# Attention's value products as one stream per pair of heads over the gate projections, half sums, and dependent loads issued later

## The chip, the cores and the metric

The kernel runs on one core of a Trainium2 chip. A core has five engines that work from queues of their own and meet through semaphores: TensorE (PE; its weight loads are listed apart as PEld), VectorE (DVE), ScalarE (ACT), GpSimd (POOL) and SyncE (SP). SP issues most of the DMAs; POOL issues a few. An engine runs its queue in order: whatever stands behind a waiting instruction waits too. The metric is the device time of one execution in microseconds (us); lower is better.

## The reference

The program is one decoder block on a sequence of 1024 tokens with 1024 features, in float32: an RMS norm with modulation, two token mixers side by side (chunkwise retention, and dilated window attention), a gated merge, and a squared-ReLU MLP. The change concerns the attention. There are three groups of heads with different dilation, four heads each, of width 128:

```python
ATT_GROUPS = ((128, 1), (512, 4), (2048, 16))
...
s = (einsum('bhrnid,bhrnjd->bhrnij', qs, kb) * (dh ** -0.5) + bias)
mx = max(s); e = exp(s - mx); den = sum(e)
p = e / den
lse = mx + log(den)
o = einsum('bhrnij,bhrnjd->bhrnid', p, vb)
...
wts = softmax(stack(lses), axis=0)
att = einsum('gbhs,gbhsd->bshd', wts, o_all)
att_out = att @ w_att_out
merged = sigmoid(gate_a) * ret_out + sigmoid(gate_b) * att_out
```

So the outputs of the three groups are weighted by a softmax over the groups' log sums, per token and head, and added. `gate_a` and `gate_b` are projections of the same normed input as queries, keys and values.

## The kernel before, in words

**Arithmetic.** Each float32 product is made of three products of parts in the shorter float32r format: a high part (a rounded copy, ScalarE) and a low part (the difference, VectorE). `mm3` (L195) issues low by high, high by low, high by high (L200, L202, L204). A weight is split by `split_w` (L190 on ScalarE, L191 on VectorE).

**Steps.** From the attention on, the work is a list of steps (`Steps`, L69). Each step has weights to load, which are issued on SP's queue (L84) as slots of a ring of three raw tiles come free, and a body. Before an ordinary step's body the weights of the next one or two steps are split; a step marked `manual` calls for that itself, at the place where its body says so. The instructions of every engine stand in the order in which the Python code emits them.

**Attention.** The heads are done in two pairs (`pair` 0 and 1); `g` is the group and `a` the head of the pair. For each pair come six key steps (`att_step`, L1692; order of groups 1, 2, 0), then gate projections as cover (`cover_step`, L1728): gates 0 to 3 for pair 0, gates 4 to 6 for pair 1, and gate 9 in `gate_step` (L1778) at the end. Every key step and gate step holds one projection of 8 chunks of six matmuls with 512 columns, into one PSUM tile of two banks (tiles `ak` and `gate`). Between the chunks lie other products:

- the scores of the previous (g, a), added to the bias into the tile `P` (L1469), their maximum, and the exponential with its sum (L1492);
- for each finished group 1 and 2, `stats_out` (L1545): the row statistics are stored in DRAM in the group's token order (`std`, L1550) and loaded back in natural order (`stn`, L1551). The load waits, on SP's queue, until the store has landed;
- after the last scores, in the first gate step, `weights` (L1553): the softmax over groups. The weights of groups 1 and 2 go through DRAM in the same way (`wtd`, L1577; `wg`, L1579). `pscale` (L1582) multiplies P by them, five of eight blocks on VectorE (L1587) and three on ScalarE (L1589);
- the products with the values. `pv_tr` (L1600) transposes up to four blocks of P on TensorE (tile `pt`, L1604) and splits them (`pth` L1608 on ScalarE, `ptl` L1609 on VectorE); `pv_mm` (L1611) multiplies by the value parts (L1628 to L1630) into an accumulator `pv`, a PSUM tile of two banks; `pv_end` (L1632) adds the accumulator into P's place (copy L1637 for group 0, add L1641 for the others) and splits the final sum for the output projection (L1646, L1647).

Projection tiles and accumulators share two PSUM tiles of two banks (`ps_mm`), so that a new accumulator waits until the one before has been read. `v_fetch` (L1515) loads the values of a group, `v_split` (L1521, L1522) splits them.

`pv` (L1650) is a generator that keeps three transposed blocks ahead of the products. `weave_pv` (L1676) sets a projection's chunks between its parts. Before the change each group is woven on its own: pair 0 has group 0 in gate 2, group 1 in gate 3, group 2 in the first key step of pair 1; pair 1 has group 0 in gate 6, and groups 1 and 2 in gate 9. The sigmoid of a gate (L1759) reads its PSUM tile at the end of its own step and is stored in DRAM (L1760).

Beside the first pair of heads, POOL's queue sums retention results from DRAM to DRAM (`result_sums`, L589): eight transfers of 2 MB, one after the other.

Of the kernel before, what the change touches and what calls it, by code (L numbers as in the profile page):

```python
# [133 lines left out]
def block_kernel(ctx, tc, io, stop=None, dbg=None):  # L134
# [677 lines left out]
    def wsplit(ap):  # L812
        return ap, split_w
# [528 lines left out]
                      [wsplit(w) for w in r_loads.get((h, c), ())], manual=True)  # L1342


    A = {}
    att_ctx = ExitStack()
    right_ctx = ExitStack()

# [196 lines left out]
    def stats_out(pair, g):  # L1545

        if g == 1:
            A["stn"] = A["p"].tile([P, 3, 8, 4], F32, tag="stn", name=f"stn{pair}")
        d = dram.tile([S, 4], F32, name=f"std{pair}{g}")
        nc.sync.dma_start(natural(d, g, 4), blocks(A["st"][:, g], g))  # L1550
        nc.sync.dma_start(A["stn"][:, g], natural(d, 0, 4))  # L1551

    def weights(pair):  # L1553

        p, st = A["p"], A["st"]
        stn = [st[:, 0], A["stn"][:, 1], A["stn"][:, 2]]
        mx = p.tile([P, 8, 2], F32, tag="mx", name=f"mx{pair}")
        wt = p.tile([P, 3, 8, 2], F32, tag="wt", name=f"wt{pair}")
        pr = p.tile([P, 3, 8, 2], F32, tag="pr", name=f"pr{pair}")
        sm = p.tile([P, 8, 2], F32, tag="ssum", name=f"ssum{pair}")  # L1560
        wg = p.tile([P, 2, 8, 2], F32, tag="wg", name=f"wg{pair}")
        nc.vector.tensor_max(mx, stn[0][:, :, 0:2], stn[1][:, :, 0:2])
        nc.vector.tensor_max(mx, mx, stn[2][:, :, 0:2])
        for g in range(3):
            nc.vector.tensor_sub(wt[:, g], stn[g][:, :, 0:2], mx)
        nc.scalar.activation(wt, wt, AF.Exp)
        for g in range(3):
            nc.vector.tensor_mul(pr[:, g], wt[:, g], stn[g][:, :, 2:4])
        nc.vector.tensor_add(sm, pr[:, 0], pr[:, 1])
        nc.vector.tensor_add(sm, sm, pr[:, 2])  # L1570
        nc.vector.reciprocal(sm, sm)
        for g in range(3):
            nc.vector.tensor_mul(wt[:, g], wt[:, g], sm)
        A["w", 0] = wt[:, 0]
        ds = [dram.tile([S, 2], F32, name=f"wtd{pair}{g}") for g in (1, 2)]
        for g in (1, 2):
            nc.sync.dma_start(natural(ds[g - 1], 0, 2), wt[:, g])  # L1577
        for g in (1, 2):
            nc.sync.dma_start(blocks(wg[:, g - 1], g), natural(ds[g - 1], g, 2))  # L1579
            A["w", g] = wg[:, g - 1]  # L1580

    def pscale(g, a):  # L1582
# [46 lines left out]
            nc.tensor.matmul(o, v[0], pl[:, cs], start=False, stop=False, skip_group_check=True)  # L1629
            nc.tensor.matmul(o, v[0], ph[:, cs], start=False, stop=True, skip_group_check=True)  # L1630

    def pv_end(pair, g, a, acc):  # L1632

        f = flat(acc)
        sumt = A["P", 0, a][:, :1024]
        if g == 0:
            nc.scalar.copy(sumt, f)  # L1637
        else:
            r = 4 * g
            sv = sumt.rearrange("p (i r) -> p r i", r=r)  # L1640
            nc.vector.tensor_add(sv, f.rearrange("p (r i) -> p r i", r=r), sv)  # L1641
# [8 lines left out]
    def pv(pair, *groups):  # L1650


        items = [(g, a, bank) for g in groups for a in range(2) for bank in PT[g]]
        accs = {}
        queue = []

        def mm(g, a, bank, pt):
            if (g, a) not in accs:
                accs[g, a] = (ps_mm(f"pv{pair}{g}{a}"), set())
            pv_mm(g, a, bank, pt, *accs[g, a])  # L1660
            if bank is PT[g][-1]:
                pv_end(pair, g, a, accs[g, a][0])
                return True
            return False

        for item in items:
            if item[2] is PT[item[0]][0]:
                del A["scaled", item[0], item[1]]
            queue.append((*item, pv_tr(pair, *item)))
            yield item is items[2]  # L1670
# [5 lines left out]
    def weave_pv(main, n, pair, *groups):  # L1676


        parts, waits = sum(4 * len(PT[g]) for g in groups), 2 * len(groups) + 1
        heavy = max(1.0, (parts - waits) / max(1, n - waits))  # L1680
        total = parts + waits * (heavy - 1)
        done = share = 0
        for wait in pv(pair, *groups):
            share += heavy if wait else 1
            while done * total < share * n:
                next(main, None)
                done += 1
        drain(main)

    combos = [(g, a) for g in (1, 2, 0) for a in range(2)]  # L1690

    def att_step(pair, i):  # L1692

        g, a = combos[i]

        def body(*args):
            ps = ps_mm(f"ak{pair}{i}")
            gen = proj_gen(ps, hd.pop("w") if i == pair == 0 else args[-1])
            if i == len(combos) - 1:
                v_fetch(pair, 0)  # L1700
            if i > 0:
                last = combos[i - 1]
                weave(gen, NK, scores_gen(pair, *last), len(SB[last[0]]), lag=2)
            elif pair == 0:
                args[0](1, True)
                for _ in range(4):
                    next(gen)
                on_T(H - 1, NC - 2)
                on_T(H - 1, NC - 1)
                drain(gen)  # L1710
                u_final(H - 1)
                result_sums()
                open_att()
                args[0](3)
            else:

                weave_pv(at(gen, 0, lambda: v_split(0, 2)), NK - 1, 0, 2)
            if i == 0:
                A["st"] = A["p"].tile([P, 3, 8, 4], F32, tag="st", name=f"st{pair}")
                bias_load(pair)  # L1720
            k_split(pair, g, a, ps)
            if i > 0:
                scores_end(pair, *last)
                if last[1] == 1:
                    stats_out(pair, last[0])
        return body

    def cover_step(pair, n):  # L1728


        i = COVER[pair][n]

        def body(*args):
            ps = ps_mm(f"gate0{i}")
            gen = proj_gen(ps, args[-1])
            if n == 0:
# [22 lines left out]
            nc.scalar.activation(t, flat(ps), AF.Sigmoid)  # L1759
            nc.sync.dma_start(gate_d[i], t)  # L1760
        return body

    for pair in range(2):
        for i, (g, a) in enumerate(combos):
            steps.add(att_step(pair, i),
                      ([] if i == pair == 0 else [wsplit(io["w_ak"][g * 4 + 2 * pair + a])]) +
                      ([(aq_d[pair, *combos[i - 1]], q_prep(pair, *combos[i - 1]))] if i > 0 else []),
                      manual=i == pair == 0)
        for n in range(len(COVER[pair])):
            more = [(aq_d[pair, *combos[-1]], q_prep(pair, *combos[-1]))] if n == 0 else []  # L1770
            steps.add(cover_step(pair, n), more + [wsplit(io["w_gate"][len(COVER[0]) * pair + n])], manual=n == 2)
# [26 lines left out]
    steps.add(gate_step, [wsplit(io["w_gate"][len(COVER[0] + COVER[1])])])  # L1798

    def open_mh():  # L1800
        hpool_ctx.close()
# [883 lines left out]
```

## Time and profile before

| | us |
|---|---|
| median of 3 runs | 2212.76 |
| lowest, highest run | 2210.62, 2216.35 |
| the profiled execution | 2214.49 |
| its span (first to last instruction) | 2212.6 |
| TensorE busy in the span | 2157.9 |
| VectorE busy | 1472.7 |
| ScalarE busy | 944.8 |

Times in the profile are counted from the span's start. The key steps of pair 0 begin at 954 us, its gate steps at 1035.8, gate 2 after 1060.6; the key steps of pair 1 follow from 1111, its gate steps from 1199.8, and the output projection of the attention (tile `ao`) from 1280.1. A row of the timeline gives start, duration, engine, line, operation, output and inputs, and in brackets the idle time before it and what ended it. A line SPq is the moment at which SP issues a DMA, not the transfer. In the page, the granted clock is that of TensorE, 1.00 being full speed.

### The profile page before, as it was taken

The numbers are of one execution on the slowest core, as the hardware profiler recorded it, in microseconds if no ns is written. First come the engines' busy times: TensorE is split into PE (matmuls) and PEld (weight loads), VectorE is DVE, ScalarE is ACT, GpSimd is POOL, SyncE is SP. The second block draws the span as 40 slices with busy tenths as digits, with TensorE's granted clock in tenths as the row PEclk, the third lists the DMA queues.
The fourth block names the chain that finished last, engine by engine and source line by source line (L and its number), as shares of the span: only waits on it lengthen the run. The fifth ranks groups of instructions, "written<-read, shape, count | busy, mean of one in ns | idle before, by whom it ended". The sixth has DMA issues, their size and how long they took to land.

```text
span 2212.6 us, 27000 instructions
## 1 busy us (share of the span) xinstructions
PE 2157.9 (98%) x10034; PEld 1787.3 (81%) x10034; DVE 1472.7 (67%) x2271; ACT 944.8 (43%) x1709; POOL 169.2 (8%) x176
## 2 busy tenths in 40 slices
PE   7999999999999999999899999999999999999998
PEld 4888888888788788888788788888878888788887
DVE  6756777766566677754555644676876665787855
ACT  4532323333234466654534634524454445533412
POOL 0100111000001233300000000002100000000003
PEclk9999999999999999999999999999999999999999
DMA  9869999744687645569523265654154445645322
GB/s 383 222 208 294 293 304 278 200 153 151 222 298 289 227 158 190 176 216 259 166 79 105 87 214 186 238 179 164 38 191 148 147 147 183 250 135 175 119 86 77
DMA packets 159906, 422.54 MB, mean 191 GB/s; under 512 B 27478, under 2 KB 55389, under 8 KB 155358
## 3 DMA queue, kind: packets, MB, share of 16 engines
q1 hardware_dynamic: 151902, 372.57, 47.5%
q0 software_dynamic: 7872, 48.24, 9.4%
q8 instruction: 79, 1.29, 0.2%
q14 instruction: 53, 0.43, 0.1%
HBM read 325.71 MB, written 160.32 MB: 220 GB/s over the span
## 4 chain that ended last, share of the span: by engine, by line
PE 85%; DVE 6%; ACT 4%; DMA 3%; issue 1%; POOL 0%; SPq 0%; POOLq 0%; DVEq 0%; ACTq 0%
PE qap L200 6%; PE qap L204 6%; PE qap L202 6%; PE fp L200 4%; PE fp L202 4%; PE fp L204 4%; PE f2a L202 2%; PE f2a L204 2%; PE f2a L200 2%; PE ak L200 2%; PE ak L202 2%; PE ak L204 2%; PE va L202 1%; PE va L204 1%; PE va L200 1%; PE rg L202 1%
## 5 line engine op out<-in xcount | busy, mean ns | idle before, releaser
L200 PE MATMUL qap<-hh,qaw 128*128 128x512 f32 x264 | 102.9, 390 | 0.2 <-DVE qat L291 0.2
L202 PE MATMUL qap<-hl,qaw 128*128 128x512 f32 x264 | 102.7, 389 | 0.0
L204 PE MATMUL qap<-hh,qaw 128*128 128x512 f32 x264 | 102.7, 389 | 0.0
L631 POOL TENSOR_TENSOR j<-qk,j 128x512 fp32r<-128x512 f32 x32 | 50.5, 1579 | 326.4 <-ACT j L630 326.4
L2140 ACT ACTIVATE a<-a 128x512 f32<-128x512 f32 x48 | 30.3, 632 | 79.3 <-DVE a L2139 79.3
L2036 POOL TENSOR_TENSOR accnf<-accnf,sqnf 128x256 f32<-128x256 f32 (+1 forms) x18 | 16.6, 922 | 613.3 <-ACT sqnf L2035 613.3
L1492 ACT ACTIVATE P<-P,ng 128x128 f32<-128x128 f32 (+1 forms) x96 | 41.9, 438 | 41.5 <-DVE ng L1489 41.5
L200 PEld LDWEIGHTS qap<-hh,qaw 128*128 128x128 f32 x264 | 49.6, 188 | 11.1 <-DVE qat L291 0.9
L204 PEld LDWEIGHTS qap<-hh,qaw 128*128 128x128 f32 x264 | 49.6, 188 | 10.4
L202 PEld LDWEIGHTS qap<-hl,qaw 128*128 128x128 f32 x264 | 49.6, 188 | 10.3
L2329 ACT CAST w2h<-w2s 128x512 fp32r<-128x512 f32 x36 | 22.4, 622 | 79.0 <-DVE w2s L2367 79.0
L257 DVE TENSOR_TENSOR fw<-w1r,fw 128x512 fp32r<-128x512 f32 x48 | 32.9, 688 | 33.3 <-ACT fw L247 33.3
L257 DVE TENSOR_TENSOR qaw<-wa,qaw 128x512 fp32r<-128x512 f32 x66 | 45.1, 687 | 12.6 <-ACT qaw L247 12.6
L2036 POOL TENSOR_TENSOR accn<-accn,sqn 128x512 f32<-128x512 f32 x12 | 15.6, 1296 | 488.6 <-ACT sqn L2035 488.6
L247 ACT CAST qaw<-wa 128x512 fp32r<-128x512 f32 x66 | 39.8, 617 | 25.3 <-PE qap L204 15.2
L200 PE MATMUL fp<-h2h,fw 128*128 128x512 f32 x128 | 50.0, 390 | 0.0
L204 PE MATMUL fp<-h2h,fw 128*128 128x512 f32 x128 | 49.8, 389 | 0.0
L202 PE MATMUL fp<-h2l,fw 128*128 128x512 f32 x128 | 49.8, 389 | 0.0
L200 PE MATMUL roa<-rh,rwl 128*128 128x512 f32 x128 | 49.8, 389 | 0.0
L202 PE MATMUL roa<-rl,rwh 128*128 128x512 f32 x128 | 49.8, 389 | 0.0
L204 PE MATMUL roa<-rh,rwh 128*128 128x512 f32 x128 | 49.8, 389 | 0.0
L1874 DVE TENSOR_TENSOR rwl<-rwl,rwh 128x1024 fp32r<-128x1024 f32 x25 | 30.2, 1221 | 29.0 <-ACT rwh L1904 29.0
(3057 smaller groups left out, 7126.3 us busy)
## 6 DMA issues: line engine op xcount, KB each, us to landing
cossin<-in_w_ada_dram SPq DMA_DIRECT2D x32, 512.0 KB, 5.1
v<-vd SPq DMA_DIRECT2D x32, 512.0 KB, 4.7
w1r<-in_w_ff_dram SPq DMA_DIRECT2D x32, 512.0 KB, 4.8
vd<-vo SPq DMA_DIRECT2D x24, 512.0 KB, 6.6
yt<-y POOLq DMA_DIRECT2D x6, 2048.0 KB, 15.0
xsd<-as SPq DMA_DIRECT2D x24, 512.0 KB, 3.0
w2r<-in_w_ff2s_dram SPq DMA_DIRECT2D x24, 512.0 KB, 7.6
em<-in_w_ada_dram SPq DMA_DIRECT2D x16, 512.0 KB, 10.2
```

The lines of the kernel that those rows point to most:

```text
L200: nc.tensor.matmul(o, wl, xh, start=first, stop=False, skip_group_check=skip)
L202: nc.tensor.matmul(o, wh, xl, start=False, stop=False, skip_group_check=skip)
L204: nc.tensor.matmul(o, wh, xh, start=False, stop=last, skip_group_check=skip)
L247: nc.scalar.copy(t[:, :512], src)
L257: nc.vector.tensor_sub(t[:, 512:], src, fv(t[:, :512]))
L631: nc.gpsimd.tensor_sub(t[:, 1], src, fv(t[:, 0]))
L1492: nc.scalar.activation(v, v, AF.Exp, bias=ng[:, blk:blk + 1], accum_out=st[:, g, blk, 2 + a:3 + a])
L1874: nc.vector.tensor_sub(lo, fv(lo), fv(hi))
L2036: (nc.vector if f == 7 else nc.gpsimd).tensor_add(G["acc", key], G["acc", key], sq)
L2140: nc.scalar.activation(o, o, AF.Relu)
L2329: nc.scalar.copy(hi, src)
```

## The change

1. `stats_out` and `weights` no longer issue the loads that depend on their own stores (`stn`, `wg`). They put them on a list, `A["later"]`, which `later_loads` issues: at the end of each key step after the first, ahead of that step's own `stats_out`, and in the second gate step. On SP's queue the loads of the next raw weights, and for `stn` of group 2 also two value loads, now stand ahead of them.
2. In the first gate step the PSUM tile is copied to SBUF (ScalarE) before the last exponentials; its sigmoid and store come at the end of the second gate step.
3. The value products of a pair are one generator over all three groups (`pv_stream`), 40 parts, of which each step takes a number: pair 0 takes 16 in gate 2, 14 in gate 3 and 10 in the next key step; pair 1 takes 20 in gate 6 and 20 in gate 9. `pscale` of groups 1 and 2 is emitted inside the stream, four items before the first transposes that need it. The new weave gives more chunks to the parts that end an accumulator (up to 1.6 more) and to the third set of transposes.
4. `pv_end` reads an accumulator bank by bank: the first half after half of the products, the second at the end.
5. The steps with value products are `manual`: the split of the next step's weights is called for at the fourth chunk, no longer before the step. The value splits of groups 1 and 2 move by a chunk or so.

The number and shapes of the matmuls and DMAs stay; ScalarE has six instructions more, VectorE eight.

```diff
         nc.sync.dma_start(natural(d, g, 4), blocks(A["st"][:, g], g))
-        nc.sync.dma_start(A["stn"][:, g], natural(d, 0, 4))
+        A["later"].append((A["stn"][:, g], natural(d, 0, 4)))
+
+    def later_loads():
+        while A["later"]:
+            nc.sync.dma_start(*A["later"].pop(0))
...
         for g in (1, 2):
-            nc.sync.dma_start(blocks(wg[:, g - 1], g), natural(ds[g - 1], g, 2))
+            A["later"].append((blocks(wg[:, g - 1], g), natural(ds[g - 1], g, 2)))
...
-    def pv_end(pair, g, a, acc):
+    def pv_end(pair, g, a, acc, hf):
         sumt = A["P", 0, a][:, :1024]
         if g == 0:
-            nc.scalar.copy(sumt, f)
+            nc.scalar.copy(sumt[:, 512 * hf:512 * hf + 512], acc[:, hf])
         else:
-            r = 4 * g
-            sv = sumt.rearrange("p (i r) -> p r i", r=r)
-            nc.vector.tensor_add(sv, f.rearrange("p (r i) -> p r i", r=r), sv)
-        if g == 2:
+            n = 2 * g
+            sv = sumt.rearrange("p (i r) -> p r i", r=2 * n)[:, n * hf:n * hf + n]
+            nc.vector.tensor_add(sv, acc[:, hf].rearrange("p (r i) -> p r i", r=n), sv)
+        if g == 2 and hf == 1:
...
+    def pv_stream(pair):
+        accs, queue = {}, []
+        def mm(g, a, i, pt):
+            if i == 0:
+                accs[g, a] = ps_mm(f"pv{pair}{g}{a}"), set()
+            pv_mm(g, a, PT[g][i], pt, *accs[g, a])
+            n = len(PT[g])
+            if i % (n // 2) == n // 2 - 1:
+                pv_end(pair, g, a, accs[g, a][0], 2 * i // n)
+            return i == n - 1
+        for k, (g, a, i) in enumerate(PV):
+            for g_, a_, i_ in PV[k:k + 4]:
+                if i_ == 0 and g_ > 0 and (g_, a_) not in accs and ("scaled", g_, a_) not in A:
+                    pscale(g_, a_)
+            queue.append((g, a, i, pv_tr(pair, g, a, PT[g][i])))
+            yield k == 2
+            if len(queue) == 3:
+                yield mm(*queue.pop(0))
+        for item in queue:
+            yield mm(*item)
...
+    def weave_pv(main, n, pair, parts):
+        first = A.get(("at", pair), 0)
+        if first == 0:
+            A["pv", pair] = pv_stream(pair)
+        flags = WAITS[first:first + parts]
+        A["at", pair] = first + parts
+        heavy = min(1.6, 0.7 * n / max(1, sum(flags)))
+        base = (n - heavy * sum(flags)) / parts
+        done, share = 0, 1e-6
+        for flag in flags:
+            assert next(A["pv", pair]) == flag
+            share += base + heavy * flag
+            while done + 1 <= share:
                 next(main, None)
                 done += 1
...
-                weave_pv(at(gen, 0, lambda: v_split(0, 2)), NK - 1, 0, 2)
+                gen = at(at(gen, 0, lambda: v_split(0, 2)), 3, lambda: args[0](3))
+                weave_pv(gen, NK - 1, 0, 10)
...
             if i > 0:
                 scores_end(pair, *last)
+                later_loads()
                 if last[1] == 1:
                     stats_out(pair, last[0])
...
                 drain(gen)
+                t = A["g0"] = ring(f"g0{i}s", F32)
+                nc.scalar.copy(t, flat(ps))
                 scores_end(pair, *combos[-1])
                 weights(pair)
                 for a in range(2):
                     pscale(0, a)
-            elif n == 1:
+                return
+            if n == 1:
                 drain(at(gen, 4, lambda: v_split(pair, 0)))
+                later_loads()
+                t = A["g0"]
+                nc.scalar.activation(t, t, AF.Sigmoid)
+                nc.sync.dma_start(gate_d[COVER[pair][0]], t)
             elif n == 2:
                 v_fetch(pair, 2)
-                gen = at(gen, 3, lambda: (args[0](3), v_split(pair, 1)))
-                weave_pv(gen, NK - 1, pair, 0)
-                for a in range(2):
-                    pscale(1, a)
+                gen = at(at(gen, 2, lambda: v_split(pair, 1)), 4, lambda: args[0](3))
+                weave_pv(gen, NK - 1, pair, (16, 20)[pair])
             else:
-                weave_pv(at(gen, 3, lambda: [pscale(2, a) for a in range(2)]), NK - 1, pair, 1)
+                weave_pv(at(gen, 3, lambda: args[0](3)), NK - 1, pair, 14)
...
-    def gate_step(w):
+    def gate_step(ahead, w):
         ps = ps_mm("gate9")
-        gen = at(proj_gen(ps, w), 2, lambda: v_split(1, 2))
-        gen = at(gen, 3, lambda: [pscale(2, a) for a in range(2)])
-        weave_pv(gen, NK - 1, 1, 1, 2)
+        gen = at(at(proj_gen(ps, w), 1, lambda: v_split(1, 2)), 3, lambda: ahead(3))
+        weave_pv(gen, NK - 1, 1, 20)
```

More of the change, by code (lines that the diff above doesn't have):

```diff
@@ L1342, in block_kernel @@
                       [wsplit(w) for w in r_loads.get((h, c), ())], manual=True)
-    A = {}
+    A = {"later": []}
     att_ctx = ExitStack()
@@ L1648, in pv_end @@
             A["att", h] = (ah, al)
[L1650 to L1670, printed above, removed]
+    PV = [(g, a, i) for g in range(3) for a in range(2) for i in range(len(PT[g]))]
+    def pv_stream(pair):
[12 more added lines that the diff above has]
+                    pscale(g_, a_)
+            if i == 0:
+                assert A["scaled", g, a]
+            queue.append((g, a, i, pv_tr(pair, g, a, PT[g][i])))
+            yield k == 2
             if len(queue) == 3:
@@ L1674, in pv, with pv_waits @@
             yield mm(*item)
[L1676 to L1685, printed above, removed]
+        for g in range(3):
+            for a in range(2):
+                del A["scaled", g, a]
+    def pv_waits():
+        ends = [(g, a, i) == (g, a, len(PT[g]) - 1) for g, a, i in PV]
+        flags = []
+        for k in range(len(PV)):
+            flags += [k == 2] + ([ends[k - 2]] if k > 1 else [])
+        return flags + ends[-2:]
+    WAITS = pv_waits()
+    def weave_pv(main, n, pair, parts):
[11 more added lines that the diff above has]
+            while done + 1 <= share:
                 next(main, None)
                 done += 1
+        if first + parts == len(WAITS):
+            drain(A["pv", pair])
         drain(main)
@@ L1767, in block_kernel @@
                       ([(aq_d[pair, *combos[i - 1]], q_prep(pair, *combos[i - 1]))] if i > 0 else []),
-                      manual=i == pair == 0)
+                      manual=i == 0)
         for n in range(len(COVER[pair])):
             more = [(aq_d[pair, *combos[-1]], q_prep(pair, *combos[-1]))] if n == 0 else []
-            steps.add(cover_step(pair, n), more + [wsplit(io["w_gate"][len(COVER[0]) * pair + n])], manual=n == 2)
+            steps.add(cover_step(pair, n), more + [wsplit(io["w_gate"][len(COVER[0]) * pair + n])], manual=n > 1)
     G = {}
@@ L1796, in gate_load @@
         nc.sync.dma_start(G[b, j], gate_d[8 * b + j])
-    steps.add(gate_step, [wsplit(io["w_gate"][len(COVER[0] + COVER[1])])])
+    steps.add(gate_step, [wsplit(io["w_gate"][len(COVER[0] + COVER[1])])], manual=True)
     def open_mh():
```

1 line of the change is left out of this document (removed).

## The prediction

> **What bounds the kernel now.** I read the page first, then who waited for whom on TensorE in the attention stretch, the chain of work there in order of time, and the stretches with the granted clock.
>
> ```profile
> span 2212.6 us, 27000 instructions
> PE 2157.9 (98%) x10034; PEld 1787.3 (81%) x10034; DVE 1472.7 (67%) x2271; ACT 944.8 (43%) x1709; POOL 169.2 (8%) x176
> ```
>
> TensorE is busy for 2157.9 of 2212.6 us. The change issues the same matmuls with the same shapes, so it can win only idle time and slow clock, and only between 1060 us (first gate step with value products) and 1280 us (end of attention). The waits of that stretch (who waited, for whom: us in all, times, longest):
>
> ```profile
> PE gate L200 <- ACT g00s L1759: 3.8, 1, 3.8
> PE pv L1628 <- DVE P L1641: 3.3, 4, 0.9
> PE pt000(0, 0, 0)_8917 L1604 <- DVE P L1587: 2.2, 1, 2.2
> PE pv L1629 <- DVE ptl010(0, 0, 0)_9136 L1609: 1.2, 1, 1.2
> PE pv L1629 <- DVE ptl110(0, 0, 0)_10475 L1609: 1.2, 1, 1.2
> ...
> PE pv L1628 <- DVE vl L1522: 0.7, 1, 0.7
> PE pv L1628 <- issue: 0.5, 1, 0.5
> ```
>
> Two of them (3.8 and 2.2) are one hole at 1061 us, in pair 0 only. The chain back from there, in order of time:
>
> ```profile
> 1039.82 10.14 DMA raw<-in_w_gate_dram
> ...
> 1051.07 1.23 DVE raw_8581l L191
> ...
> 1057.11 3.94 ACT P L1492 x16
> 1061.05 0.14 ACT wt L1566
> ...
> 1062.49 2.50 ACT P L1589 x6
> ...
> 1071.30 0.47 PE gate L200 x2
> ...
> 1072.67 0.12 PE pv L1628
> ```
>
> A gate weight lands late (1039.82 + 10.14); VectorE's queue stands behind its split; the last score sums, exponentials (1057.11) and scaling by the softmax weights (1062.49) follow late; ScalarE reaches the sigmoid that frees a PSUM tile last. (1071.30 to 1072.67: one projection chunk of six matmuls is 1.37 us.) The weight was issued late because SP's queue stood behind a load that waits for its own store:
>
> ```profile
> 1029.20 0.33 SPq L1550 DMA_DIRECT2D std<-st  x1
> 1039.35 0.38 SPq L1551 DMA_DIRECT2D stn<-std  x1
> ...
> 1062.55 4.08 SPq L1577 DMA_DIRECT2D wtd<-wt  x2
> 1074.74 3.95 SPq L1579 DMA_DIRECT2D wg<-wtd  x2
> ```
> ```profile
> 1193.06 0.33 SPq L1550 DMA_DIRECT2D std<-st  x1
> 1194.47 0.38 SPq L1551 DMA_DIRECT2D stn<-std  x1
> ...
> 1221.05 0.99 SPq L1577 DMA_DIRECT2D wtd<-wt  x2
> 1225.58 3.61 SPq L1579 DMA_DIRECT2D wg<-wtd  x2
> ```
>
> The same store takes 10.15 us in pair 0 and 1.41 in pair 1. In pair 0 the DMA engines also carry POOL's sums of retention results:
>
> ```profile
> 1063.90:1070.70 6.80, 3.32 (x11) 2.64 (x11) 3.57 (x8) 6.77 (x9) 0.00 (x0) 0.52 0.84 199
> 1070.00:1072.00 2.00, 2.00 (x13) 1.77 (x12) 2.00 (x3) 2.00 (x5) 0.00 (x0) 0.89 0.00 0
> 1272.10:1275.50 3.40, 2.52 (x22) 2.55 (x22) 1.96 (x2) 1.05 (x1) 0.00 (x0) 0.96 0.85 328
> 1275.50:1278.90 3.40, 3.40 (x11) 2.87 (x11) 2.04 (x1) 0.48 (x1) 0.00 (x0) 0.54 0.00 0
> ```
>
> (Columns: stretch, us, busy PE, PEld, DVE, ACT, POOL, granted clock, DMA share, GB/s.) The clock is near half after the hole and again at 1275.5; the DMA engines are empty from 1070.
>
> **The change part by part.** Pair 1 has the same steps without the late weight, so it gives pair 0's times by an offset:
>
> ```profile
> 1035.83 0.62 PE L200 MATMUL gate<-hh,raw_8380l 128*128 128x512 f32 x2
> ...
> 1073.22 0.49 PE L1604 MATMUL pt000(6, 1, 6)_8963<-ct,P 128*128 128x128 f32 x3
> ```
> ```profile
> 1199.75 0.62 PE L200 MATMUL gate<-hh,raw_9719l 128*128 128x512 f32 x2
> ...
> 1224.49 0.60 PE L1604 MATMUL pt100(0, 0, 0)_10256<-ct,P 128*128 128x128 f32 x4
> ...
> 1230.11 0.38 PE L1628 MATMUL pv<-pth100(0, 0, 0)_10261,vl 128*128 128x256 f32 x1 [0.31 <-ACT pth100(0, 0, 0)_10261 L1608]
> ...
> 1231.65 0.49 PE L1604 MATMUL pt100(6, 1, 6)_10302<-ct,P 128*128 128x128 f32 x3
> ```
> ```profile
> 1208.50 1.03 ACT L190 CAST raw_9920h<-raw 128x1024 fp32r<-128x1024 f32 x1
> ...
> 1219.45 0.23 ACT L1566 ACTIVATE wt<-wt 128x48 f32<-128x48 f32 x1
> 1220.99 2.51 ACT L1589 ACTIVATE P<-P,wt 128x256 f32<-128x256 f32 x6 [1.31 <-DVE wt L1573]
> ...
> 1229.48 0.58 ACT L1608 CAST pth100(0, 0, 0)_10261<-pt100(0, 0, 0)_10256 128x512 fp32r<-128x512 f32 x1
> ```
>
> The offset is 1199.75 − 1035.83 = 163.92 us. In pair 0 the tile slot that the late weight waits for is free when its last reader ends:
>
> ```profile
> 1030.15 1.23 DVE L1430 SCALAR_TENSOR_TENSOR ql<-raw,qh 128x1024 fp32r<-128x1024 f32 x1 [4.21 <-ACT qh L1429]
> ```
>
> 1. *Loads behind stores.* The two `stn` loads (L1551) and two `wg` loads (L1579) of each pair go behind later SP entries. In pair 0 the gate weight then follows the store directly. It can be issued at 1030.15 + 1.23 = 1031.4 and, even with the old 10.14, lands by 1042; it is wanted at 1208.50 − 163.92 = 1044.6, when ScalarE has finished the earlier exponentials and splits it. Pair 0 then runs as pair 1 did: first value products done at 1231.65 − 163.92 = 1067.73 instead of 1073.22. **Gain 5.5 us.** The entries let past also include SP's next raw weight, two value loads and, for `wg`, a 512 KB load; nobody waits for the gate stores behind `wg` before the retention output.
>
> 2. *Gate 0's PSUM copied first, sigmoid a step later.* One ScalarE copy of 1024 columns per pair (about 1.0 us, as the other 1024-column copies), in the idle time before the second exponentials (the tile is read straight after its projection). But before the first transposed block can be copied ScalarE still does the same 6.0 us in both versions (end of scaling, 1220.99 + 2.51 = 1223.50, to 1229.48: table load, two sigmoids, one weight copy, two value copies); only their order differs. So readiness does not move. The new weave puts three transposes and then only **one** projection chunk before the first product in pair 1 (two before the change, and two still in pair 0): 1.37 us less is done by 1231.65. **Loss 1.4 us in pair 1**, as one stall of 2.9 us up to 1230.11 and one of 0.5.
>
> 3. *One stream per pair, weights of the next step split at the fourth chunk.* The 1.2 us waits for ptl010 and ptl110 come when a step begins with two weight splits and a sigmoid ahead of the products' conversions; in the stream the conversions run on. The value split wait (0.7) moves behind a chunk, and so does the 0.5. Gain 1.2 + 0.7 in pair 0, 1.2 + 0.5 in pair 1. The split now comes some 10 us before its step ends; if that cover goes, a split costs 1.2 us (1051.07 row).
>
> 4. *Sums by halves.*
>
> ```profile
> L1641 DVE TENSOR_TENSOR P<-pv,P x8: 1983/2033/2241, 1101.3 to 1276.3; 128x1024 f32<-128x1024 f32 x8
> ```
>
> A half is about 1.1 us (half of 2033 ns and a little fixed time). The first half runs under products, and the second has one or two chunks (1.4 to 2.7 us) after it before the next accumulator starts: the four waits (3.3 us, two in each pair) go, gain 1.65 per pair. Eight more VectorE and six more ScalarE instructions lie beside TensorE.
>
> 5. *New waits.* (a) Scaling of group 1 now stands in ScalarE's and VectorE's queues between conversions, and waits for `wg`. In pair 0 the weights are ready 163.92 before 1221.05, at 1057.1; with pair 0's own 12.2 us from `wtd` to `wg` (1074.74 − 1062.55) and 4 for issue it lands near 1073; ScalarE wants it at about 1072.5 (1067.7 and a product, a chunk, a transpose and two value copies: 1.0 + 1.4 + 0.4 + 2.0). Bounds 0 to 5 us (landing as late as before, 1074.74 + 4); TensorE is two products and two chunks ahead there; I take 0.3. (b) the gate PSUM tile of step 3 waits for the sigmoid of step 2: 0.3. (c) In the last step of pair 1, VectorE has the second half sum behind a scaling (1.0 us) and two conversions when the next accumulator wants its tile: 0 to 1.8, I take 1.5. So 0.6 in pair 0 (a and b) and, with 0.5 for small ones, 2.0 in pair 1.
>
> 6. *Clock.* A half-rate stretch of 3.4 us costs 3.4 × (1 − 0.54) = 1.6. Shown are one after 2.2 us idle and one after 0.9 us idle among 128-column products, none after the 1.2 us for ptl110. So pair 1's 2.9 us stall will cost 1.6; pair 0's 1.6 + 0.5 us (two chunks end near 1064.6, product at 1066.2) half of that, 0.8; bounds 0 and 1.6 each. The stretch at 1275.5 followed a half-sum wait: its 1.6 is gained.
>
> The Trainium skill, "TensorE: Matmul & The Clock Gate", section "HAM oscillation — how this bites in real kernels", asks for no TensorE idle gap above about 3.4 us. By that, none of the new stalls would slow the clock and the sum would be 2.4 us larger; the trace disagrees (clock 0.54 after a stretch with 2.52 of 3.40 us busy), so I go by the rows.
>
> **Sum.** Pair 0: 5.5 + 1.9 + 1.65 − 0.6 − 0.8 = 7.65. Pair 1: −1.4 + 1.7 + 1.65 − 2.0 − 1.6 + 1.6 = −0.05. Together 7.6 us: 2214.49 − 7.6 = 2206.9 for the profiled execution, which lies 1.73 above the median of 2212.76; so **2205.2 us** (−0.34%). About 0.3%, 6.6 us, is what a measurement can tell from no change.
>
> **Rivals.**
>
> *A. More gain: the clock does not drop and the last step has no new wait.* Against it: the two slow stretches above. 2.4 + 1.5 + 1.0 more: 2200.3 us.
>
> *B. Given back.* `wg` lands at 1079 in pair 0 and blocks both queues (5 us of wait, 3 to 4 on TensorE), or the gate weight gains nothing because POOL's transfers hold it until 1050 whatever its place (5.5 less). For it: DMA share 0.84 still at 1063.9. Against it: the store alone did move. Left: 2 to 4 us of gain, 2209 to 2211 us.
>
> *C. Slower: the late `stn` load.* In SP's order the group 2 `stn` now stands behind three weights and two value loads. It is free up to about 1055.5, when the second exponentials end (1219.45 − 163.92); each later us costs one. If POOL's transfers hold it until the engines empty at 1070, scaling ends 3.9 later (1061.05 to 1062.49 + 2.50), first products 8.15 after that (1223.50 to 1231.65): 1082.1 against 1073.22. That is 8.9 lost for 5.5 gained, and a whole slow stretch (0.8 more): 7.6 − 15.2 = −7.6, so 2212.76 + 7.6 = 2220.4 us. The whole gain is gone once `stn` lands at about 1063. Against it: only POOL's queue competes, and pair 0's store, under the same load, needed 10.15.
> The Trainium skill, "DMA: Bandwidth & Descriptors", section "Queues, rings and completion order", says that a DMA engine takes turns between its queues packet by packet, so that a transfer of many small pieces would have to share every turn with POOL's. That speaks for C; the 10.15 against 1.41 us of the same store agrees.
>
> **How the numbers follow.** Forecast 0.58 (2202 to 2209; 0.35 of it beyond 6.6 us), A 0.12, B 0.21, C 0.09. Faster by over 0.3%: 0.35 + 0.12 = 0.47; within: 0.23 + 0.21 = 0.44; slower: 0.09. The range leaves out C and the ends of A: 2199.5 to 2213.
>
> **What would show it.** Right: no TensorE wait above 2.5 us near 1061; the gate weight issued near 1031; products from 1066; half clock after pair 1's start; no wait of pv for P; pair 0's attention ends 7 to 8 us earlier, pair 1's takes as long as before. Wrong: `stn` or `wg` landing late with ACT and DVE idle before the scaling; a half sum still awaited; no slow stretch.

## The result, and the profile after

The changed kernel takes 2234.45 us in the median (2233.85 to 2238.23, 4 runs) against 2213.9 us for the kernel before (4 runs): 1.0099 times as long, with a 95% interval of 1.0083 to 1.0115. The forecast was 2205.2 us, with a range up to 2213.0. The profiled execution took 2238.23 us, its span is 2236.1 us, 23.5 more than before.

Nearly all of it arises in the attention. The first fence has the kernel before, from the first gate step to the end of pair 0 and from there to the output projection; the second fence has the same two stretches of the changed kernel (columns as in the prediction: stretch, us, busy PE, PEld, DVE, ACT, POOL, granted clock, DMA share, GB/s).

```profile
1035.83:1131.06 95.23, 85.76 (x485) 72.82 (x484) 51.90 (x94) 45.22 (x93) 1.68 (x2) 0.96 0.54 161
1131.06:1280.09 149.03, 144.02 (x798) 123.23 (x797) 83.78 (x133) 73.32 (x171) 0.00 (x0) 0.99 0.30 93
```
```profile
1037.83:1140.39 102.56, 91.19 (x485) 77.81 (x484) 53.25 (x100) 46.29 (x95) 1.67 (x2) 0.92 0.62 153
1140.39:1301.08 160.69, 149.80 (x798) 128.29 (x796) 83.93 (x138) 73.84 (x173) 0.00 (x0) 0.95 0.28 86
```

Pair 0 takes 7.3 us more, pair 1 11.7; the stretch from the output projection to the next block takes 1.6 more, and 2.9 lie elsewhere (2.0 of them ahead of the gate steps, where nothing was changed). The number of matmuls is the same, but TensorE is busy for 11.2 us longer (91.19 + 149.80 against 85.76 + 144.02): more than half of the 19 us lost in the attention is slow clock, the rest is 7.8 us more idle time. Who waited for whom on TensorE in the attention of the changed kernel (us in all, times, longest; the lines are those of the changed kernel: L1632 to L1634 are the products with the values, L1612 and L1613 the splits of the transposed blocks, L1640 the copy and L1644 the add of `pv_end`, L1593 the scaling on ScalarE, L1555 the later loads):

```profile
PE pv L1632 <- DVE P L1644: 9.1, 4, 2.8
PE pv L1632 <- ACT P L1640: 7.4, 4, 6.5
PE pv L1632 <- ACT pth100(0, 0, 0)_10269 L1612: 2.8, 1, 2.8
PE pv L1632 <- ACT pth000(0, 0, 0)_8923 L1612: 1.4, 1, 1.4
```

The waits that step 3 of the prediction named (ptl010, ptl110, the value split, `issue`) are gone. In their place stand waits for P at L1640 and L1644, the half sums that should have ended the waiting. The timeline of TensorE shows where:

```profile
1086.13 0.58 PE L1632 MATMUL pv<-pth001(0, 0, 0)_8999,vl 128*128 128x256 f32 x1 [6.55 <-ACT P L1640]
...
1131.68 0.44 PE L1632 MATMUL pv<-pth021(4, 0, 4)_9378,vl 128*128 128x128 f32 x1 [2.62 <-DVE P L1644]
...
1239.47 0.39 PE L1632 MATMUL pv<-pth100(0, 0, 0)_10269,vl 128*128 128x256 f32 x1 [2.79 <-ACT pth100(0, 0, 0)_10269 L1612]
...
1265.64 0.35 PE L1632 MATMUL pv<-pth110(4, 0, 4)_10472,vl 128*128 128x256 f32 x1 [1.81 <-DVE P L1644]
...
1275.68 0.55 PE L1632 MATMUL pv<-pth111(4, 0, 4)_10561,vl 128*128 128x256 f32 x1 [2.83 <-DVE P L1644]
...
1292.55 0.45 PE L1632 MATMUL pv<-pth121(4, 0, 4)_10684,vl 128*128 128x128 f32 x1 [1.79 <-DVE P L1644]
```

The products that wait for VectorE are all the first of an accumulator's *second* half (block 4 on). They write the other bank of the accumulator than the one that the half sum reads; still they carry a wait for it. And that sum is late, because VectorE has other work ahead of it. The next fence is VectorE around the last of these waits: the half sum of 1291.34 stands behind `al`, which waits for ScalarE's `ah`, and that for the sum before.

```profile
1287.85 1.23 DVE L1644 TENSOR_TENSOR P<-pv,P 128x512 f32<-128x512 f32 x1 [1.01 <-PE pv L1634]
1290.19 1.23 DVE L1650 TENSOR_TENSOR al<-P,ah 128x1024 fp32r<-128x1024 f32 x1 [1.11 <-ACT ah L1649]
1291.34 1.06 DVE L1644 TENSOR_TENSOR P<-pv,P 128x512 f32<-128x512 f32 x1
```

The 6.55 us wait is of another kind: the first product of the second accumulator of group 0 waits for the PSUM tile of the first. SP's queue and ScalarE's:

```profile
1059.11 0.99 SPq L1581 DMA_DIRECT2D wtd<-wt  x2
1063.80 0.33 SPq L84 DMA_DIRECT2D raw<-aqd  x1
1071.51 11.29 SPq L1555 DMA_DIRECT2D wg<-wtd  x2
```
```profile
1083.93 1.20 ACT L1593 ACTIVATE P<-P,wg 128x256 f32<-128x256 f32 x3 [8.74 <-DMA wg<-wtd]
1085.03 0.56 ACT L1612 CAST pth001(2, 1, 2)_9022<-pt001(2, 1, 2)_9017 128x512 fp32r<-128x512 f32 x1
1085.50 0.58 ACT L1640 COPY P<-pv 128x512 f32<-128x512 f32 x1
```

There are two stores and two loads, one for group 1 and one for group 2. Group 1's store took 12.4 us (1059.11 to 1071.51), its load `wg` another 12.4 (to 1083.93). The 11.29 in the row of the loads is not the time of a transfer: the second load was issued only at 1082.47, because SP waited until the second store had landed. The scaling of group 1 waits for group 1's load and holds up the copy of group 0's second half sum (1085.50), and with it the next accumulator. After most of these waits comes half clock:

```profile
1134.80:1138.20 3.40, 3.40 (x9) 2.64 (x8) 2.04 (x2) 1.05 (x1) 0.00 (x0) 0.50 0.47 155
...
1277.00:1280.40 3.40, 3.40 (x14) 3.14 (x15) 1.68 (x2) 0.59 (x1) 0.00 (x0) 0.50 0.02 5
...
1294.00:1297.40 3.40, 3.40 (x13) 2.92 (x13) 1.10 (x1) 0.89 (x1) 0.00 (x0) 0.50 0.00 0
```

### The profile page after: what moved, and what is told of

It is laid out like the page before. It is cut to its first block, busy times and chain, and to the rows that moved or that the text cites. A ratio compares the mean times of both kernels' runs of the same rounds, so it can differ in the third digit from the quotient of the medians.

```text
span 2236.1 us, 27027 instructions
## 1 busy us (share of the span) xinstructions
PE 2170.7 (97%) x10034; PEld 1799.1 (80%) x10034; DVE 1474.1 (66%) x2279; ACT 947.7 (42%) x1715; POOL 169.3 (8%) x176
## 4 chain that ended last, share of the span: by engine, by line
PE 85%; DVE 6%; ACT 4%; DMA 3%; issue 1%; POOL 0%; SPq 0%; POOLq 0%; DVEq 0%; ACTq 0%
PE qap L200 6%; PE qap L202 5%; PE qap L204 5%; PE fp L200 4%; PE fp L202 4%; PE fp L204 4%; PE f2a L200 2%; PE f2a L204 2%; PE f2a L202 2%; PE ak L200 2%; PE ak L202 2%; PE ak L204 2%; PE rg L202 1%; PE rg L200 1%; PE rg L204 1%; PE va L202 1%
## 5 line engine op out<-in xcount | busy, mean ns | idle before, releaser
L1275 DVE SCALAR_TENSOR_TENSOR cossin<-cossin,cb 128x1024 f32<-128x1024 f32 x32 | 39.0, 1219 | 15.8 <-DMA cossin<-in_w_ada_dram 15.8
```

The source lines that it names most:

```text
L1275: nc.vector.scalar_tensor_tensor(t, t, 1.0, cb, op0=ALU.mult, op1=ALU.mult, accum_out=mods[:, j:j + 1])
```

## The experiments

Two theories stood at the start: the half sums block the second half of their own accumulator (W), or VectorE's queue is simply too late, with halves or without (Q). For the wait in pair 0: the place of the scaling in the stream (G), or the transfers of POOL that make `wg` late (P). Ratios are times against the kernel before, taken in the same set of runs; 0.1% is 2.2 us. The median of the kernel before went from 2207.5 to 2213.9 us between the sets, so times of different sets are compared by their ratios. "Attention" is the time from the first matmul of gate 0 to the first of the output projection in the profiled execution: 244.26 before, 263.25 after.

### Whole sums, and two halves at the end

```diff
-            if i % (n // 2) == n // 2 - 1:
-                pv_end(pair, g, a, accs[g, a][0], 2 * i // n)
+            if i == len(PT[g]) - 1:
+                pv_end(pair, g, a, accs[g, a][0])      # the whole sum, as before
```
```diff
-            if i % (n // 2) == n // 2 - 1:
-                pv_end(pair, g, a, accs[g, a][0], 2 * i // n)
+            if i == n - 1:
+                pv_end(pair, g, a, accs[g, a][0], 0)
+                pv_end(pair, g, a, accs[g, a][0], 1)
```

> The changed kernel with the accumulators read whole again, after the last product; all else as changed. Theory W (a half sum blocks the second half's products, because the wait is on the whole accumulator tile): the waits of pv for the sums inside an accumulator (9.1 us for VectorE's sums and 0.85 of the small ones for ScalarE's) go, and most of the half-rate stretches after them (about 3.2 us in pair 0, 6.5 in pair 1); in their place come waits of about 0.8 us at the next accumulator's start, as before. 10 to 14 us faster than the changed kernel: 2221 to 2225 us. Theory Q (VectorE's queue is late there, because the value splits, the scaling and the next step's weight split now stand in it; the halves do not matter): the same waits come back at the next accumulator's start, within 4 us of the changed kernel, 2230 to 2238. The 6.5 us wait in pair 0 stays in both.

> The changed kernel, with the two half sums kept as two instructions but both emitted after the last product of the accumulator. Theory W (a half sum costs because the second half's products wait for it): within 2 us of the run with whole sums, 2217 to 2222 us. Rival (the additional instructions or their form cost): near the changed kernel, 2229 us or more.

Measured: whole sums 2218.79 us, ratio 1.0040 (1.0026 to 1.0054); two halves at the end 2216.06 us, 1.0035 (1.0020 to 1.0049). So 0.6%, some 13 us of the 22, hang on the first half sum's place alone: with the same two instructions at the end, they are gone. TensorE's waits with whole sums:

```profile
PE pv L1632 <- ACT P L1641: 5.8, 1, 5.8
PE pv L1632 <- DVE P L1645: 3.0, 3, 1.3
```

VectorE's sums cost 3.0 us again, as before the change (3.3), and pair 1 falls from 160.69 to 146.46 us. W holds, Q falls. Whether the chip needs that wait, or the program's bookkeeping of whole tiles sets it, was not tried: it would take accumulators of two separate tiles.

### The scaling later, and both edits

```diff
-            for g_, a_, i_ in PV[k:k + 4]:
+            for g_, a_, i_ in PV[k:k + 2]:
```

> The changed kernel with the scaling of a group's P put into the stream two items ahead of its use, not four; all else as changed. Theory G (the scaling of group 1 waits for its weights wg, which land at 1084 us, and holds ScalarE's copy of group 0's sum and three conversions behind it): the 6.5 us wait at 1086 us falls below 2 us and the half-rate stretch after it goes, 6 to 9 us faster than the changed kernel, 2225 to 2229 us; pair 1, where wg is early, stays within 1.5 us. Rival: with the wait out of the way TensorE reaches the same landing time of wg a few instructions later and waits there: under 3 us gained, 2231 to 2235.

> Both edits in the changed kernel: whole sums, and the scaling two items ahead. If the two causes are all of the loss and add up (12 and 8 us of 21): 2212 to 2217 us, level with the kernel before. If the two causes overlap or a third one is at work (the order of the splits, the one chunk before the first product in pair 1, the clock): above 2219.

Measured: the scaling later alone 2227.58 us, 1.0078 (1.0063 to 1.0093); with whole sums 2214.35 us, 1.0018 (1.0007 to 1.0028). The 6.5 us wait is gone (ScalarE's sums cost 1.2 us in all, the longest 0.7), and the two edits add up: 0.59% and 0.21% alone, 0.81% together. G holds, but for less than the 6 to 9 us expected: 4 to 5 us, with intervals that overlap those of the runs without it. Pair 1 did not stay within 1.5 us either: it takes 162.95 us in place of 160.69, and with whole sums 149.14 in place of 146.46. There the transposes now wait for the scaling, which is emitted only just ahead of them:

```profile
PE pt120(0, 0, 0)_10599 L1608 <- DVE P L1591: 1.1, 1, 1.1
```

Some 4 us are left.

### One projection chunk more ahead of the first product in pair 1

```diff
-        done, share = 0, 1e-6
+        done, share = 0, 0.1 if (pair, first) == (1, 0) else 1e-6
```

> The run with whole sums and the scaling two items ahead (ratio 1.0018), and in pair 1 two projection chunks before the first product instead of one. If the prediction's step 2 is right (the missing chunk is a stall of 2.8 us and a slow stretch of 1.7 us, of which the chunk fills 1.4): the wait for pth100 falls to 1.4 us and the half-rate stretch after it goes or shrinks, 1.5 to 3 us faster, ratio 1.0003 to 1.0011. Rival (the chunk is missed later, at the next accumulator): ratio 1.0015 to 1.002, with larger waits later in that step.

Measured, with the two edits above: 2212.08 us, 1.0007 (0.9996 to 1.0018). The wait for pth100 went from 2.8 to 1.4 us, the 1.4 us that step 2 of the prediction had charged for the missing chunk. Pair 1 went from 149.14 to 147.73 us, but whole sums alone, with one chunk, had 146.46, so that the equal size there is partly luck; and the intervals of the two ratios overlap. What is left, 0.07%, can't be told from none. One wait that the kernel before doesn't have stands in all versions of the stream, behind the output projection; no run takes it away:

```profile
PE roa L200 <- DVE g L1871: 1.4, 1, 1.4
```

### Part 1 alone, and the kernel before once more

The kernel before with `stn` and `wg` on the list, issued where the change issues them:

```diff
-        nc.sync.dma_start(A["stn"][:, g], natural(d, 0, 4))
+        A["later"].append((A["stn"][:, g], natural(d, 0, 4)))
...
-            nc.sync.dma_start(blocks(wg[:, g - 1], g), natural(ds[g - 1], g, 2))
+            A["later"].append((blocks(wg[:, g - 1], g), natural(ds[g - 1], g, 2)))
```

> The kernel before with part 1 alone: stn and wg put on the list and issued later; products, sums, gate 0 and splits as before. If the late gate weight was what made pair 0's hole, and wg has its cover when group 1 is scaled only after all products of group 0: the gate 2 step starts near 1062 instead of 1067.4 and pair 0 ends 4 to 6 us earlier, 2207 to 2210 us. If wg, which landed at 1084 in the changed kernel, is still too late for the scaling at the end of gate 2 (about 1084): half of it is given back, 2210 to 2212. If the later loads themselves cost: above 2214.

> A second profile of the kernel before, because its hole in pair 0 (3.8 and 2.2 us of waits, gate 2 at 31.6 us after gate 0) is known from one execution only. Theory V (the hole depends on where POOL's transfers stand when the store of the statistics is issued, so it varies from execution to execution): another size of the hole, 0 to 6 us, with the start of POOL's last transfer moved against gate 0 by some us. Rival (it is set by the order of the queues alone): the hole is the same within 1 us.

Measured: part 1 alone 2211.69 us, 1.0002 (0.9993 to 1.0011), though its attention takes 238.25 us, 6.0 less than the profile before. The second profile of the kernel before (2208.20 us) shows why the 6.0 say little:

```profile
PE pv L1628 <- DVE P L1641: 3.4, 4, 0.9
PE gate L200 <- ACT g00s L1759: 2.7, 1, 2.7
```

There is no wait for pt000, and the hole is 2.7 us in place of 6.0; its attention takes 239.37 us, 4.9 less than in the first profile. The hole that the prediction wanted to close is half as large in another execution. So the attention is 6.0 us shorter with part 1 than in the one profile and 1.1 shorter than in the other, and the whole time shows nothing. That the size varies (V) is shown. Its cause is not: POOL's last transfer started 14.4 us after gate 0 in the first profile (1050.22 to 1035.83) and 17.8 us in the second (1054.60 to 1036.85), later where the hole is smaller.

### POOL's sums moved in the program

```diff
-                result_sums()                     # first key step of pair 0
...
+            if (pair, i) == (1, 1):
+                result_sums()
```

> The changed kernel with POOL's retention sums started in the second key step of pair 1 instead of the first of pair 0. Theory P (POOL's transfers make the small stores and loads of pair 0 slow, and with them wg late): store and load of the weights take under 3 us each in place of 12.4, the 6.5 us wait and its slow stretch go, 7 to 11 us faster than the changed kernel, 2220 to 2226 us. Rival: the transfers meet the loads of pair 1 instead (its wg is stored at about 1230, some 100 us after the transfers start), pair 1 grows by as much, 2228 us or more. The waits for half sums stay in both.

> The kernel before with part 1 alone and POOL's retention sums started in the second key step of pair 1. Theory P: pair 0 then runs like pair 1 without a late weight, gate 0 of pair 0 to the output projection takes 236 us or less (244.3 before, 238.3 with part 1 alone), 2203 to 2208 us. Rival: the transfers meet pair 1's loads or those of the output projection: 2209 us or more.

Measured: 2227.86 us, 1.0093 (1.0078 to 1.0108), and with part 1 alone 2208.75 us, 1.0005 (0.9995 to 1.0014): nothing moved. POOL's queue holds nothing else there, and the first transfer started as ever:

```profile
971.48 0.60 POOL L581 DMA_DIRECT2D yt<-y  x1 [16.40 <-DMA y<-on]
```

So the two are second measurements of the changed kernel and of part 1 alone. In this profile of the former the wait for group 0's sum is 2.9 us, and the attention takes 256.17: here, too, one execution shows several us more than another.

### POOL's sums held back

POOL first reads a column of `wg` of pair 0; its transfers come behind that in its queue. Three ways to do it, on three kernels each: into a new tile of 4 bytes, a new tile of 64 bytes, or a dead tile (`mx`).

```diff
+                if pair == 0:                     # second gate step, behind later_loads()
+                    hold = cst.tile([P, 1], F32, name="hold")
+                    nc.gpsimd.tensor_tensor(hold, A["w", 2][:, 0, 0:1], mhalf[:, 0:1], op=ALU.add)
+                    result_sums()
```

> The changed kernel with POOL's retention sums really begun later: POOL first reads one column of pair 0's weights wg, so its eight transfers start after wg has landed and run under the rest of pair 0 and the key steps of pair 1. (In the run before, only the place in the program moved; POOL's queue was empty and the transfers started at 971 us all the same.) Theory P (POOL's transfers make pair 0's small stores and loads slow): the store of the softmax weights takes 1 to 3 us in place of about 12, wg lands before 1070, the wait of 3 to 6.5 us for group 0's sum goes, 4 to 8 us less than the changed kernel: ratio 1.006 to 1.008. Rival (the small transfers are slow by themselves in pair 0, or wait behind SP's own value loads): wg lands past 1075, ratio 1.009 or more.

> The kernel before with part 1 alone, and POOL's sums held until pair 0's wg has landed. Theory P: no hole is left in pair 0, gate 0 of pair 0 to the output projection in 236 to 238 us; against the kernel before in the mean (239.4 us in its second profile) 2 to 4 us faster: ratio 0.998 to 0.999. Rival: the transfers now meet the key steps and loads of pair 1 and give it back: ratio 1.000 or more.

> Whole sums, scaling two items ahead, two chunks before the first product of pair 1, and POOL's sums held until pair 0's wg has landed: all causes found so far taken away, with the one stream, gate 0's copy and the later splits kept. If these are all the causes: level with the kernel before or better, ratio 0.998 to 1.0005. If the stream itself costs (the order of scaling and conversions in VectorE's queue, the 1.4 us wait behind the output projection): 1.001 or more.

Measured with 4 bytes: 1.0128 (1.0106 to 1.0150), 1.0072 (1.0058 to 1.0086), 1.0071 (1.0057 to 1.0085). All three are slower than without the hold (1.0099, 1.0002 and 1.0007; the first with intervals that overlap), with a *shorter* attention (251.68, 237.18, 235.86 us). The loss lies behind it: one matmul of the output projection, in the kernel before and then in part 1 with the hold:

```profile
L200 PE MATMUL ao<-ah,raw_9932l 128*128 128x512 f32 x16 | 4.9, 389 | 0.0
```
```profile
L200 PE MATMUL ao<-ah,raw_9933l 128*128 128x512 f32 x16 | 5.0, 396 | 0.0
```

> As the changed kernel with POOL's sums held until pair 0's wg has landed, but the tile that POOL writes for it is 64 bytes per partition in place of 4. If the 4 bytes made the later matmuls slow: they take 389 ns again, and what is left is the hold's own worth: the wait for group 0's sum in pair 0 gone, 4 to 8 us less than the changed kernel, ratio 1.005 to 1.008. Rival (the transfers themselves, now under pair 1, or something else of the hold slow the matmuls): 396 ns again, ratio 1.012 to 1.014.

> The kernel before with part 1 and the hold, tile of 64 bytes. By the first of the two: 389 ns, attention in 236 to 238 us as with 4 bytes, ratio 0.998 to 0.9995 (about 240 us in the mean before). By the rival: 1.007 again.

> Whole sums, scaling two items ahead, two chunks first in pair 1, the hold, tile of 64 bytes. By the first: attention in 236 us as with 4 bytes, less the 1.4 us wait behind the output projection: ratio 0.998 to 1.000, level with the run above within 0.1%. By the rival: 1.007 again.

With 64 bytes 1.0133 (1.0120 to 1.0146), 1.0052 (1.0040 to 1.0064), 1.0063 (1.0051 to 1.0075), and the same matmul at

```profile
L200 PE MATMUL ao<-ah,raw_9933l 128*128 128x512 f32 x16 | 5.0, 394 | 0.0
```

So it was not the 4 bytes as such. What both tiles have in common is their place: they lie in the pool `cst`, which the kernel opens ahead of the pools of the weights (`wraw`, `whl`), while `ah` and `al` lie in a pool on the other side of SBUF (`side="right"`). A new tile there may move the weights against `ah` and `al`. That is argued from the order of the pools; no run on record shows the addresses.

> The changed kernel with POOL's sums held until pair 0's wg has landed, the column written into a dead tile, so that no tile moves in SBUF. If the shift of the tiles slowed the matmuls: 389 ns from the output projection on; attention as in the two runs with the hold (251.7 us with the 4-byte tile, 256 to 263 without the hold): ratio 1.005 to 1.008. If the hold itself does: 394 to 396 ns, ratio 1.012 or more.

> The kernel before with part 1 and the hold, no tile moved. By the shift: 389 ns, attention in 237 us, 2 to 3 us less than the kernel before in the mean, ratio 0.998 to 0.9995. By the hold: 1.005 or more.

> Whole sums, scaling two items ahead, two chunks first in pair 1, and the hold, no tile moved. By the shift: attention in 236 us and 1.4 us of wait behind the output projection, ratio 0.998 to 1.000. By the hold: 1.005 or more.

Without a new tile: 2223.21 us, 1.0067 (1.0046 to 1.0088); 2208.81 us, 0.9998 (0.9989 to 1.0006); 2211.03 us, 1.0010 (1.0000 to 1.0020), with 389 ns. So it was the new tile, and not the hold or the transfers under pair 1. (Nor the chip: the run with two chunks and no hold, of the same set as those with 4 bytes, has 389 ns.) That the tile acts by the shift fits, but isn't shown. And the hold's own effect is now to be seen, on SP's queue and on POOL of the changed kernel with the hold:

```profile
1060.71 0.99 SPq L1581 DMA_DIRECT2D wtd<-wt  x2
1065.39 0.33 SPq L84 DMA_DIRECT2D raw<-aqd  x1
1065.82 3.46 SPq L1555 DMA_DIRECT2D wg<-wtd  x2
```
```profile
1072.42 0.19 POOL L1778 TENSOR_TENSOR mx<-wg,ct 128x1 f32<-128x1 f32 x1 [114.11 <-DMA wg<-wtd]
```

The trip of the weights takes 11.7 us (1060.71 to 1072.42) in place of at least 24.8, although SP's own load of 512 KB (1065.39) stands ahead of `wg` here too. The wait for group 0's sum in pair 0 falls to 0.3 us. Pair 0 of the changed kernel takes 90.54 us in place of 102.56 and 96.80. In the second execution without the hold the two ways were shared out otherwise:

```profile
1057.88 16.81 DMA wtd<-wt
...
1074.71 4.28 DMA wg<-wtd
```

P holds: POOL's transfers made `wg` late. The sizes expected were off (the store in 1 to 3 us, `wg` before 1070). That they do it by sharing turns is not shown. P agrees with the Trainium skill, "DMA: Bandwidth & Descriptors", section "Queues, rings and completion order" (an engine's queues take turns packet by packet).

The hold helps the changed kernel alone: 1.0067 against 1.0099 and 1.0093. The other two kernels missed the gains expected of it, with 0.9998 (against 1.0002 and 1.0005 without it) and 1.0010 (against 1.0007). The kernel before with part 1 and the hold has the shortest attention with the old steps, 237.12 us, but 0.9998 is no gain that can be told from none; no version here beats the kernel before.

## Why the prediction was wrong, step by step

- **Step 1 (late weight, 5.5 us): mechanism right, worth less.** The gate weight was issued at 1033.34 (forecast 1031.4), and gate 2 starts 25.97 us after gate 0 in place of 31.55: 5.6 us. But the second profile of the kernel before has 27.99 without any change, and part 1 alone moved the time by nothing that shows (1.0002). The step was worked out on an execution with a long hole and then counted against the median.
- **Step 2 (1.4 us lost in pair 1): right.** The stall was forecast as 2.9 and 0.5 us; it was 2.79 and 0.34. In pair 0, 1.6 and 0.5 forecast, 1.40 and 0.34 measured. The additional chunk took 1.4 off the stall.
- **Step 3: right**; none of the four waits is left.
- **Step 4 (sums by halves, +1.65 per pair): the step that failed.** It followed the second half only ("the first half runs under products") and did not ask who waits for the first half's read. The next products of the same accumulator do, although they write its other bank. Four waits for whole sums of 3.3 us became waits for half sums inside the accumulators and their slow clock: 13 us in the runs.
- **Step 5a (`wg`, 0.3 us): failed in size.** Its place and its two blocked queues were named; the landing was forecast at 1073, with a bound of 1078.7, and came at 1083.9. The sum took 12.2 us for the store, as in the profile before, and 4 for the load. In the profiled execution they took 12.4 and 12.4 under POOL's transfers, in the second one 16.8 and 4.3: one profile of the kernel before did not show how far this varies. In the runs it cost 4.6 us by the scaling's place (1.0099 to 1.0078) and 7 by the hold (to 1.0067), with intervals that overlap the changed kernel's.
- **Step 5c** put a wait of 1.5 us for a second half sum at the last accumulator's start. There is none there; the waits of the last step (2.83, 1.79) are for first halves.
- **Step 6 (clock): right per stall, wrong in the sum.** Half clock followed six stalls (1.40, 6.55, 2.62, 2.79, 2.83 and 1.79 us), not two, and mostly for more than the 3.4 us that were charged (the step's own row at 1063.90 already has 6.80 us at 0.52); only the stall of 1.81 us at 1265.64 was followed by full clock. The Trainium skill, "TensorE: Matmul & The Clock Gate", section "HAM oscillation — how this bites in real kernels", asks for no gap above about 3.4 us; the rows after 1275.68 and 1292.55 disagree again, with 0.50 after stalls of 2.83 and 1.79. The stretch at 1275.5 before the change followed the wait for a whole sum (0.9 us), not for a half.
- **The rivals.** B named the wait for `wg`, but as a loss out of a gain. C did not happen, though narrowly: VectorE goes on from its last maxima to the operation that reads `stn` (1053.55) without a wait, and by the landing times in the trace `stn` had come at 1053.51. That a half sum blocks its own accumulator was on no list.

## What to carry to other kernels

If a read is split so that work can go on beside it, follow both ends: whoever writes the same tile next may wait for the read of the first part, and in an in-order queue that read comes after everything emitted ahead of it. A scaling that waits for a DMA does not belong ahead of copies that free PSUM; emitted too late, it makes its own readers wait. Before a gap in one profile is counted as gain, look at a second profile: here the gap was half as large.

## What the runs showed that was not expected

- A new tile of 4 or 64 bytes per partition in the first pool made the matmuls of the output projection take 396 and 394 ns in place of 389, and the whole time 0.5 to 0.7% longer. Whether it does so by moving tiles on one side of SBUF against those on the other was not shown, and which relation of the addresses would matter was not tried.
- Idle time cost more than as much again in clock: 7.8 us more of idle in the attention came with 11.2 us more of busy time for the same matmuls.
- The store and the load of the softmax weights (8 KB for each group) took 12.4 and 12.4 us, or 16.8 and 4.3 us, for group 1 beside POOL's transfers of 2 MB. Without them both groups' stores and loads took 11.7 us together.
